# Low parts of 32 chunks of u made early, kept in DRAM, and moved by GpSimd's queue

## The chip, the cores and the metric

The kernel runs on one core of a Trainium2 chip. The metric is the time of one execution in microseconds of the device, from the runs shown below. The engines are TensorE (PE, its weight loads PEld), VectorE (DVE), ScalarE (ACT), GpSimd (POOL) and SyncE (SP), which only issues transfers. Each engine takes its instructions from a queue in a fixed order and waits at the head of it. GpSimd, ScalarE and SyncE can also issue DMAs from their queues.

## What is computed

Two blocks of a transformer for 512 tokens of width 1024, all in float32. The first block has a mixer (latent attention and retention, both gated and merged) and then a PEER layer: each token picks 16 experts of 16384 in each of 8 heads, by a top-16 over two sets of 128 keys, and adds up what they give. The second block has an attention with three branches and an ordinary feed-forward layer. The lines that matter here are

```python
merged = jax.nn.sigmoid(za) * y_a + jax.nn.sigmoid(zr) * y_r     # the merges
...
act = jax.nn.gelu(jnp.einsum('td,tkd->tk', xt, peer_u[it]), approximate=False)
return jnp.einsum('tk,tkd->td', gt * act, peer_v[it])
```

## The kernel before

**Products in three passes.** Float32 accuracy is kept by cutting each operand into a high part `h` in the reduced float32r type and a low part `l`, the remainder. A product is three matmul passes: high by high, high by low, low by high (`fm`, L256 for its matmuls). `weights` (L224) fetches a weight tile of 128 x 1024 by SP's queue into `wr`; `split` (L210, L211) makes `wh` by a cast on ScalarE and `wl` by a subtract, on VectorE or GpSimd. `wr`, `wh` and `wl` have two buffers each. For the mixer's weights (`wfm`) the subtract goes to GpSimd every second time.

**The merges.** For each of the 8 chunks of 128 output columns the loop before L860 makes four products: the gate `w_za`, the attention's `w_mla` (half as long), the gate `w_zr`, the retention's `w_ret`. `merged` then adds the two gated results (L856, GpSimd), and makes the high and low part of half the sum (ScalarE, VectorE). The residual product `w_mix` and the query products follow.

**Routing, with early fronts beside it.** PEER is computed for all experts: 128 chunks of 128 experts. For the first 384 tokens a `front` multiplies one chunk of `u` with the tokens (24 matmuls) and takes the gelu; later a chunk of `v` is multiplied with the gated activations. The last 128 tokens are done apart, by gathering the rows of `u` and `v` with indirect DMAs on GpSimd. 72 of the 128 fronts stand beside the routing: VectorE finds the top 16 and writes one-hot tables (`topk`, `spread`, L928 to L1096), ScalarE scales them, TensorE multiplies them (L1101) into the gate table, which goes to DRAM. `step` (PACE, LEAD) sets how many fronts have been traced after each step of the routing. In these fronts the chunk's low part is always made by GpSimd:

```python
def front(e, u=None):
    u = u or u_of(e, G)
```

From front 72 on, fronts alternate with the products of `v`, in a loop whose order on three engines is written out by hand; there the low part is VectorE's.

**What sets the order.** In the merges and in the routing, the order of each engine's queue is laid out when the program is built, by a planner that walks through the traced instructions with costs of its own, puts an instruction into its engine's queue when its inputs and its tile are ready there, and prefers what was traced earlier. On the chip the queues are then followed as they are. A tile's buffer is handed on when its last reader has finished.

Of the kernel before, what the change touches and what calls it, by code (L numbers as in the profile page):

```python
# [9 lines left out]
F32 = mybir.dt.float32  # L10
F32R = mybir.dt.float32r
# [3 lines left out]
OP = mybir.AluOpType  # L15
AX = mybir.AxisListType

P = 128
# [4 lines left out]
D = 1024  # L23
KD = D // P
# [142 lines left out]
def build(tc, A, OUT):  # L167
    nc = tc.nc
    es = ExitStack()
    V, S, G, TE = nc.vector, nc.scalar, nc.gpsimd, nc.tensor  # L170

    def pool(name, bufs=1, stack=es, **kw):
        if kw.get("space") != bass.MemoryType.DRAM:
            kw["reuse_waits"] = "tile"
        return stack.enter_context(tc.tile_pool(name=name, bufs=bufs, **kw))

    cp = pool("cst")
    dp = pool("dram", space=bass.MemoryType.DRAM)
# [10 lines left out]
    def mmps(name="mm"):  # L189
        return bank("mm", name)  # L190
# [17 lines left out]
    def split(src, hi, lo, lo_eng=None):  # L208

        S.copy(hi, src)  # L210
        (lo_eng or V).tensor_tensor(lo, src, hi.bitcast(F32), op=OP.subtract)  # L211
# [6 lines left out]
    def load(ap, n, tag="w", queue=nc.sync):  # L218
        wp, words, bufs = wts[tag]
        raw = wp.tile([P, words], F32, name=tag + "r", bufs=bufs)  # L220
        queue.dma_start(raw[:, :n], ap)
        return raw

    def weights(ap, n, lo_pool=3, tag="w", raw=None):  # L224

        wp, words, bufs = wts[tag]
        raw = raw or load(ap, n, tag)
        hi = wp.tile([P, words], F32R, name=tag + "h", bufs=2)
        lo = wp.tile([P, words], F32R, name=tag + "l", bufs=2)
        flip[0] += 1  # L230
        if isinstance(lo_pool, int):
            lo_pool = V if flip[0] % lo_pool else G
        split(raw[:, :n], hi[:, :n], lo[:, :n], lo_pool)
        return hi, lo

    def kview(pair, kt, width):
        return tuple([t[:, k * width:(k + 1) * width] for k in range(kt)] for t in pair)
# [55 lines left out]
    def ks(t):  # L293

        return [t[:, k] for k in range(t.shape[1])]
# [131 lines left out]
    def two(tp, name="t2", dt=F32):  # L427

        return tp.tile([P, L], dt, name=name, tag="t2")
# [4 lines left out]
    def halves(name, tag, dt=F32):  # L434
        h = [xp.tile([P, 4, L], dt, name=name, tag=tag, bufs=2) for _ in range(2)]
        return h, [h[k // 4][:, k % 4] for k in range(KD)]
# [18 lines left out]
    def half_slot(name, dt=F32):  # L455
        return sp_.tile([P, 4, L], dt, name=name, tag="h")

    def flat(t, n):
        return t.rearrange("p k t -> p (k t)")[:, :n]

    def mtwo(name="m2"):
        return tp.tile([P, L], F32, name=name, tag="m2", bufs=9)

    src = A["hT"].rearrange("p (k t) -> p k t", k=KD)
    _, h1 = halves("h1", "xa")
# [56 lines left out]
    c = ks(half_slot("ckv", F32R))  # L522
# [6 lines left out]
    x = mtwo()  # L529
# [8 lines left out]
    for t0, t1, m in ((0, NT, P), (NT, NT + 1, M)):  # L538
        h = t1 - t0
        pv = pt[:m, t0 * 32:t1 * 32].rearrange("p (t d) -> p t d", t=h)  # L540
        x = mtwo()
# [84 lines left out]
    for h in range(8):  # L626
        b = 64 - h % 2 * 64
# [4 lines left out]
    def fm_pieces(w, pieces):  # L632

        x = two(t2)
        for a, b in pieces:
            ps = mmps()
            fm(ps[:, :b - a], w, hn, 0, a, b - a)
            S.copy(x[:, a:b], ps[:, :b - a])
        return x
# [110 lines left out]
    for h in range(8):  # L750
        x = fm_pieces(wfm("w_rv", h), PIECES)
# [10 lines left out]
        b = h % 2 * 64  # L762
# [65 lines left out]
    for h in range(8):  # L828
        w = wfm("w_rg", h)
# [10 lines left out]
    def gate(name, c, x):  # L840

        w = wfm(name, c)
        ps = mmps()
        fm(ps, w, hn, 0, 0, T)
        S.activation(x, ps, AF.Tanh, scale=0.5)
        return x

    def gated(name, c, act, kt, x):

        w = wfm(name, c, kt)  # L850
        ps = mmps()
        fm(ps, w, act, 0, 0, T, kt)
        V.scalar_tensor_tensor(x, x, 1.0, ps, op0=OP.add, op1=OP.mult)

    def merged(a, b, mg, d):
        G.tensor_tensor(a, a, b, op=OP.add)  # L856
        S.activation(mg[0][d], a, AF.Copy, scale=0.5)
        V.scalar_tensor_tensor(mg[1][d], a, 0.5, mg[0][d].bitcast(F32), op0=OP.mult, op1=OP.subtract)

    mg = tuple([x for _ in range(2) for x in ks(half_slot(n, F32R)[:, :, :T])] for n in ("mgh", "mgl"))  # L860
    for c in range(KD):
        x = gate("w_za", c, two(t2)[:, :T])
        gated("w_mla", c, oT, 4, x)
        y = gate("w_zr", c, two(t2)[:, :T])
        gated("w_ret", c, yr, KD, y)
        merged(x, y, mg, c)
    sty.close()
    h1 = [x for _ in range(2) for x in ks(half_slot("h1"))]
# [69 lines left out]
    acts, done_u = {}, []  # L938

    def u_of(e, eng=V):  # L940
        return kview(weights(A["u_T"][e], D, eng), KD, P)

    def act_tile(e, side):
        return (tr if side else tp).tile([P, TD], F32, name="act", bufs=15 if side else 19)
# [381 lines left out]
    for x in range(2):  # L1326
# [8 lines left out]
        for hf in range(2):  # L1335
            w = sp_.tile([P, 8, 256], F32, name="wc1", tag="h")
            nc.sync.dma_start(w.rearrange("p l c -> p (l c)"), A["w_c1"][x][:, hf * 2048:(hf + 1) * 2048])
            w1.append(w)
    for br in range(2):
        w = wfm("w_kv", 2 * br)  # L1340
# [4 lines left out]
        for g in range(2):  # L1345
            a, b = slice(g * 64, g * 64 + 64), slice(64 - g * 64, 128 - g * 64)
# [4 lines left out]
        w = wfm("w_kv", 2 * br + 1)  # L1351
        ps = mmps()
        fm(ps, w, hn, 0, 0, T)
        x = two(t2)[:, :T]
# [8 lines left out]
    w = wfm("w_gn", 0, width=48)  # L1363
# [3 lines left out]
    x = two(t2)[:48, :T]  # L1367
# [158 lines left out]
    for g in range(4):  # L1526
        w = wfm("w_u", g)
# [32 lines left out]
    for c in range(KD):  # L1560
        y = gate("w_gm", KD + c, two(t2)[:, :T])
        gated("w_pn", c, ysl, KD, y)
        x = gate("w_gm", c, two(t2)[:, :T])
# [19 lines left out]
    w = kview(weights(A["w_f1"][0], KD * 256, tag="ww"), KD, 256)  # L1583
# [11 lines left out]
    for b in range(4):  # L1595
        f = tuple(ks(slot(n, F32R)) for n in ("fh", "fl"))
        for c in range(4):
            if b or c:
                w = kview(weights(A["w_f1"][4 * b + c], KD * 256, tag="ww"), KD, 256)
# [52 lines left out]
```

## Time and profile before

| what | value |
|---|---|
| time, median of 3 runs | 2685.57 us (2683.2 to 2687.15) |
| the profiled execution | 2681.29 us |
| its span | 2679.5 us |
| TensorE busy | 2585.8 us, 97% |
| VectorE, ScalarE, GpSimd busy | 1702.9, 1146.1, 926.6 us |
| moved by DMA | 465.80 MB |

The span is what the profile covers; the execution takes 1.8 us more. TensorE's matmuls overlap and their ends are modelled, so that its busy share is no measure of how much room is left; waits and the chain of waits are. The merges fill about 344 to 500 us of the span, the routing about 605 to 1014, the fronts with the products of `v` follow to about 1805, and then comes the second block.

### The profile page before, as it was taken

To read this page: it belongs to the slowest core of one execution; us is meant where nothing else is said; L and a number is where in the kernel's file an instruction comes from. 1 tells how busy PE (TensorE), PEld (TensorE's weight loads), DVE (VectorE), ACT (ScalarE), POOL (GpSimd) and SP (SyncE) were. 2 spreads that over 40 slices of the span, in tenths; PEclk is the share of its full clock that TensorE was granted. 3 is DMA by queue.
4 is the path that set the end of the run, shared out by engine and by line. 5 is a ranking of instruction groups with operands and counts; after the bars stand their busy time and mean duration, and the time that the engine had idled before them with its cause. 6 is when DMAs were issued, how large, how long until landed. Compare 5 with 4: busy or idle time off the path is not lost.

```text
span 2679.5 us, 37137 instructions
## 1 busy us (share of the span) xinstructions
PE 2585.8 (97%) x13809; PEld 2225.1 (83%) x13809; DVE 1702.9 (64%) x3399; ACT 1146.1 (43%) x2097; POOL 926.6 (35%) x590
## 2 busy tenths in 40 slices
PE   8899999999899999999999999999999999899998
PEld 7768778899899988888888888887666788787887
DVE  5772442246998992898989888866778412534333
ACT  5552342244577663333333333334667422422322
POOL 2122122325344342565555555522222233211112
PEclk9999999999999999999999999998999999999999
DMA  3322223323356568999999999963110122222221
GB/s 129 100 69 68 67 75 122 119 84 118 103 174 195 168 199 290 331 368 400 402 408 370 339 351 333 337 203 108 53 43 25 60 95 96 109 94 95 94 95 63
DMA packets 177957, 465.80 MB, mean 174 GB/s; under 512 B 15856, under 2 KB 78960, under 8 KB 171120
## 3 DMA queue, kind: packets, MB, share of 16 engines
q1 hardware_dynamic: 136736, 322.84, 34.7%
q0 software_dynamic: 36864, 134.23, 13.6%
q10 hardware_dynamic: 4176, 6.36, 0.8%
q8 instruction: 108, 1.77, 0.3%
q14 instruction: 73, 0.60, 0.1%
HBM read 421.17 MB, written 37.42 MB: 171 GB/s over the span
## 4 chain that ended last, share of the span: by engine, by line
PE 78%; DVE 14%; ACT 2%; DMA 2%; issue 2%; POOL 1%; ACTq 1%; SPq 0%; DVEq 0%; POOLq 0%
PE mm L256 36%; PE py L1182 19%; PE pu L256 13%; DVE oh L1093 3%; PE o L1510 2%; PE tp L1505 1%; DMA t<-t 1%; PE mm L1101 1%; DVE xn L350 1%; DVE oh L1065 1%; DVE oh L1068 1%; DVE oh L1096 1%; PE s L699 1%; DVE ef L1070 1%; DMA wr<-in_u_T_dram 1%
## 5 line engine op out<-in xcount | busy, mean ns | idle before, releaser
L211 POOL TENSOR_TENSOR wl<-wr,wh 128x1024 fp32r<-128x1024 f32 (+1 forms) x142 | 349.9, 2465 | 764.5 <-ACT wh L210 329.5
L210 ACT CAST wh<-wr 128x1024 fp32r<-128x1024 f32 (+2 forms) x271 | 273.4, 1010 | 311.2 <-PE mm L256 203.4
L256 PE MATMUL pu<-xf,wh 128*128 128x384 f32 x2048 | 392.3, 343 | 10.3 <-ACT wh L210 5.8
L256 PEld LDWEIGHTS pu<-xf,wh 128*128 128x128 f32 x2048 | 362.0, 190 | 16.3 <-ACT wh L210 6.2
L211 DVE TENSOR_TENSOR wl<-wr,wh 128x1024 fp32r<-128x1024 f32 (+2 forms) x129 | 152.0, 1179 | 184.0 <-ACT wh L210 112.2
L974 POOL DMA_INDIRECT row<-in_v_rows_dram,eg x128 | 195.7, 1529 | 163.7 <-DVE yg L989 136.9
L974 POOL DMA_INDIRECT row<-in_u_rows_dram,eg x128 | 187.8, 1467 | 176.2 <-DVE row L979 155.1
L256 PE MATMUL pu<-xf,wl 128*128 128x384 f32 x1024 | 202.4, 339 | 2.6 <-POOL wl L211 2.6
L1169 ACT CAST ah<-act 128x384 fp32r<-128x384 f32 x128 | 65.8, 514 | 324.0 <-DVE act L1166 302.2
L1182 PE MATMUL py<-vl,ah 128*128 128x512 f32 x768 | 195.8, 389 | 0.1
L1182 PE MATMUL py<-vh,ah 128*128 128x512 f32 x768 | 195.7, 389 | 0.0
L1182 PE MATMUL py<-vh,al 128*128 128x512 f32 x768 | 195.6, 389 | 0.0
L256 PEld LDWEIGHTS pu<-xf,wl 128*128 128x128 f32 x1024 | 182.5, 189 | 3.5 <-POOL wl L211 3.5
L1174 DVE TENSOR_TENSOR vl<-vr,vh 128x1024 fp32r<-128x1024 f32 x128 | 156.3, 1221 | 22.3 <-ACT vh L1172 22.3
L1182 PEld LDWEIGHTS py<-vl,ah 128*128 128x128 f32 x768 | 144.0, 188 | 30.6 <-DVE vl L1174 0.7
L1182 PEld LDWEIGHTS py<-vh,al 128*128 128x128 f32 x768 | 144.2, 188 | 30.0
L989 DVE SCALAR_TENSOR_TENSOR yg<-row,ag,yg 128x1024 f32<-128x1024 f32 x127 | 162.9, 1282 | 5.3 <-DMA row<-in_v_rows_dram,eg 2.9
L1182 PEld LDWEIGHTS py<-vh,ah 128*128 128x128 f32 x768 | 143.3, 188 | 25.4
L979 DVE SCALAR_TENSOR_TENSOR row<-row,xg 128x1024 f32<-128x1024 f32 x128 | 152.3, 1221 | 9.9 <-DMA row<-in_u_rows_dram,eg 9.9
L1093 DVE TENSOR_TENSOR oh<-iota,eT 128x1024 f32<-128x1024 f32 x96 | 139.8, 1483 | 14.0 <-PE mm L1101 12.6
L381 DVE TENSOR_TENSOR h<-mm,h 128x512 f32<-128x512 f32 (+1 forms) x54 | 34.1, 632 | 172.6 <-PE mm L256 172.6
L1172 ACT CAST vh<-vr 128x1024 fp32r<-128x1024 f32 x128 | 134.6, 1051 | 19.5 <-PE py L1182 18.7
(468 smaller groups left out, 5103.3 us busy)
## 6 DMA issues: line engine op xcount, KB each, us to landing
wr<-in_u_T_dram SPq DMA_DIRECT2D x128, 512.0 KB
vr<-in_v_rows_dram SPq DMA_DIRECT2D x128, 512.0 KB
wwr<-in_w_f_dram SPq DMA_DIRECT2D x32, 1024.0 KB
gates<-stg SPq DMA_DIRECT2D x24, 1024.0 KB
gin<-gates SPq DMA_DIRECT2D x16, 1536.0 KB
wr<-in_w_gm_dram SPq DMA_DIRECT2D x16, 512.0 KB
ahead<-act SPq DMA_DIRECT2D x41, 192.0 KB
act<-ahead SPq DMA_DIRECT2D x41, 192.0 KB
```

What stands on the lines that cost most here:

```text
L210: S.copy(hi, src)
L211: (lo_eng or V).tensor_tensor(lo, src, hi.bitcast(F32), op=OP.subtract)
L256: TE.matmul(out, w[a][k][:, c0:c0 + P], act[b][k][:, t0:t0 + n], start=i == 0 and k == 0, stop=i == 2 and k == kt - 1)
L974: G.indirect_dma_start(out=r, out_offset=None, in_=src, in_offset=bass.IndirectOffsetOnAxis(ap=eg[:, k:k + 1], axis=0))
L979: V.scalar_tensor_tensor(r, r, 1.0, xg, op0=OP.mult, op1=OP.mult, accum_out=ag[:, k:k + 1])
L989: V.scalar_tensor_tensor(yg[0], r, ag[:, k:k + 1], yg[0], op0=OP.mult, op1=OP.add)
L1093: V.tensor_tensor(a1, iota[:, None, None, :].to_broadcast([P, 2, 4, P]), eT[:, :2, b0 + q0:b0 + q0 + 4, None].to_broadcast([P, 2, 4, P]), ...
L1169: S.copy(ah, a)
L1172: S.copy(vh, raw)
L1174: V.tensor_tensor(vl, raw, vh.bitcast(F32), op=OP.subtract)
L1182: TE.matmul(py[2 * t + d], x[:, t * P:(t + 1) * P], w[:, d * 512:(d + 1) * 512], start=e == 0 and i == 0, stop=e == P - 1 and i == 2)
L1510: TE.matmul(po[b * 64:b * 64 + 64, :2 * P], vt[:, j, br, g], pT[:, b * 256:b * 256 + 256], start=False, stop=last, skip_group_check=True)
```

## The change

For the 32 even chunks 0, 2, ... 62 of `u`, the low part is made during the merges and stored in DRAM (`ulow`, 32 x 512 KB). Four staging buffers are used: each holds a chunk and, beside it, its high part. `low_load` fetches a chunk on GpSimd's queue; `low_part` casts it (ScalarE), subtracts (VectorE), stores the remainder to `ulow` on GpSimd's queue, and fetches the chunk four further on into the same buffer. One `low_part` stands behind each of the four products of a merge round. In `front`, `weights` then takes the low part of these chunks from `ulow`, by a DMA on GpSimd's queue, in place of the subtract; the chunk itself is still fetched and cast. The add in `merged`, which both blocks use, goes from GpSimd to VectorE.

```diff
-    def weights(ap, n, lo_pool=3, tag="w", raw=None):
+    def weights(ap, n, lo_pool=3, tag="w", raw=None, low=None):
...
+        if low is not None:
+            G.dma_start(lo.bitcast(F32)[:, :n], low)
+            S.copy(hi[:, :n], raw[:, :n])
+            return hi, lo
...
     def merged(a, b, mg, d):
-        G.tensor_tensor(a, a, b, op=OP.add)
+        V.tensor_tensor(a, a, b, op=OP.add)
...
+    NLOW = 32
+    low_of = {2 * j: j for j in range(NLOW)}
+    ulow = dp.tile([NLOW, P, D], F32, name="ulow")
...
+    stage = [flat(x, 2 * D) for x in halves("stage", "xa")[0] + [half_slot("stage") for _ in range(2)]]
+
+    def low_load(j):
+        G.dma_start(stage[j % 4][:, :D], A["u_T"][2 * j])
+
+    def low_part(j):
+        raw, hi = stage[j % 4][:, :D], stage[j % 4][:, D:].bitcast(F32R)
+        S.copy(hi, raw)
+        V.tensor_tensor(raw.bitcast(F32R), raw, hi.bitcast(F32), op=OP.subtract)
+        G.dma_start(ulow[j], raw)
+        if j + 4 < NLOW:
+            low_load(j + 4)
+
+    for j in range(4):
+        low_load(j)
     for c in range(KD):
         x = gate("w_za", c, two(t2)[:, :T])
+        low_part(4 * c)
         gated("w_mla", c, oT, 4, x)
+        low_part(4 * c + 1)
         y = gate("w_zr", c, two(t2)[:, :T])
+        low_part(4 * c + 2)
         gated("w_ret", c, yr, KD, y)
+        low_part(4 * c + 3)
         merged(x, y, mg, c)
...
     def u_of(e, eng=V):
-        return kview(weights(A["u_T"][e], D, eng), KD, P)
+        return kview(weights(A["u_T"][e], D, eng, low=ulow[low_of[e]] if e in low_of else None), KD, P)
```

## Rows read from the trace of the kernel before

**Rows 1.** Chain that ended last, shares of the span by engine and by line.

```profile
PE 78%; DVE 14%; ACT 2%; DMA 2%; issue 2%; POOL 1%; ACTq 1%; SPq 0%; DVEq 0%; POOLq 0%
PE mm L256 36%; PE py L1182 19%; PE pu L256 13%; DVE oh L1093 3%; PE o L1510 2%; PE tp L1505 1%; DMA t<-t 1%; PE mm L1101 1%; DVE xn L350 1%; DVE oh L1065 1%; DVE oh L1068 1%; DVE oh L1096 1%; PE s L699 1%; DVE ef L1070 1%; DMA wr<-in_u_T_dram 1%
```

**Rows 2.** Busy us by stretch: length, PE, PEld, DVE, ACT, POOL, clock, DMA share, GB/s.

```profile
344.50:500.40 155.90, 154.74 (x686) 125.01 (x685) 43.01 (x68) 50.15 (x67) 42.11 (x26) 1.00 0.31 103
605.00:1014.00 409.00, 388.48 (x2430) 382.60 (x2429) 360.28 (x982) 252.67 (x561) 179.82 (x67) 0.98 0.54 163
1300.00:1500.00 200.00, 200.00 (x960) 175.71 (x960) 179.32 (x236) 72.97 (x99) 111.93 (x76) 1.00 1.00 385
```

**Rows 3.** Waits of PE, 605 to 1045: total us, times, longest.

```profile
PE tp L1079 <- DVE ef L1070: 6.8, 1, 6.8
PE pu L256 <- ACT wh L210: 5.8, 1, 5.8
PE mm L1101 <- ACT oh L1098: 4.7, 6, 1.8
PE pu L256 <- ACT act L961: 4.4, 4, 1.7
PE pu L256 <- POOL wl L211: 2.6, 2, 2.4
PE mm L1101 <- DVE oh L1096: 2.0, 4, 0.6
```

**Rows 4.** PE in order of time in the routing: start, us, instructions merged.

```profile
609.96 2.96 PE L256 MATMUL pu<-xf,wh 128*128 128x384 f32 x16
612.75 1.57 PE L256 MATMUL pu<-xf,wl 128*128 128x384 f32 x8
614.16 2.96 PE L256 MATMUL pu<-xf,wh 128*128 128x384 f32 x16
...
684.11 4.26 PE L256 MATMUL pu<-xf,wh 128*128 128x384 f32 x15
```

**Rows 5.** GpSimd's subtract, 605 to 1014: by line, and ns min/median/max.

```profile
L211 POOL TENSOR_TENSOR wl<-wr,wh 128x1024 fp32r<-128x1024 f32 x67 | 180.4, 2693 | 229.6 <-ACT wh L210 134.3 <-PE pu L256 57.0 <-PE mm L1101 29.5
L211 POOL TENSOR_TENSOR wl<-wr,wh x67: 2361/2402/5736, 604.5 to 1011.6; 128x1024 fp32r<-128x1024 f32 x67
```

**Rows 6.** VectorE by line, 605 to 1014: busy us, mean ns, idle before.

```profile
L1093 DVE TENSOR_TENSOR oh<-iota,eT 128x1024 f32<-128x1024 f32 x96 | 139.8, 1483 | 14.0 <-PE mm L1101 12.6 <-ACT oh L1098 1.5
L1096 DVE TENSOR_SCALAR oh<-oh,eT 128x128 f32<-128x128 f32 x64 | 30.0, 526 | 0.0
L1068 DVE TENSOR_TENSOR oh<-oh,idf 128x1024 f32<-128x1024 f32 x16 | 22.7, 1425 | 0.0
```

**Rows 7.** The same lines of VectorE: ns min/median/max, first and last start.

```profile
L1093 DVE TENSOR_TENSOR oh<-iota,eT x96: 1198/1214/3429, 688.2 to 1003.9; 128x1024 f32<-128x1024 f32 x96
L1096 DVE TENSOR_SCALAR oh<-oh,eT x64: 263/278/2435, 913.1 to 1005.4; 128x128 f32<-128x128 f32 x64
```

**Rows 8.** GpSimd's indirect gather of 128 rows of u: ns min/median/max.

```profile
L974 POOL DMA_INDIRECT row<-in_u_rows_dram,eg x128: 936/1673/1989, 1014.2 to 1395.1; - x128
```

**Rows 9.** SP's queue in order of time: loads of u, start and us.

```profile
604.01 3.18 SPq L221 DMA_DIRECT2D wr<-in_u_T_dram  x2
...
1021.15 2.97 SPq L221 DMA_DIRECT2D wr<-in_u_T_dram  x2
```

**Rows 10.** ScalarE in order of time: the casts that waited for these loads.

```profile
608.98 1.05 ACT L210 CAST wh<-wr 128x1024 fp32r<-128x1024 f32 x1 [4.33 <-DMA wr<-in_u_T_dram]
...
1033.01 1.04 ACT L210 CAST wh<-wr 128x1024 fp32r<-128x1024 f32 x1 [3.27 <-DMA wr<-in_u_T_dram]
```

**Rows 11.** By line, 344.5 to 500.4, engines ACT, DVE, POOL.

```profile
L210 ACT CAST wh<-wr 128x1024 fp32r<-128x1024 f32 x24 | 25.2, 1050 | 40.1 <-PE mm L256 36.3 <-DMA wr<-in_w_za_dram 3.8
L211 DVE TENSOR_TENSOR wl<-wr,wh 128x1024 fp32r<-128x1024 f32 x15 | 18.4, 1225 | 45.2 <-PE mm L256 45.2
L856 POOL TENSOR_TENSOR t<-t,t 128x512 f32<-128x512 f32 x7 | 9.1, 1295 | 0.0
```

## The prediction

> **What bounds the kernel now.** I read the chain of waits first [rows 1]: TensorE holds 78% of it and VectorE 14%, and the VectorE lines in it (L1093, L1065, L1068, L1096, L1070) all belong to one stage, the routing with the 72 early fronts. Then I cut the span into the two stages that the change touches [rows 2]. During the merges (344.5 to 500.4) TensorE is busy for 154.7 of 155.9 us at a granted clock of 1.00, while GpSimd works 42 us, ScalarE 50, VectorE 43, and the DMA engines have a share of 0.31. So the merges are TensorE's, 155.9 / 8 = 19.5 us for each of eight rounds, with much room beside it. In the routing stage (605 to 1014) TensorE is busy 388.5 of 409 us and VectorE 360.3: two engines that lead in turn. What TensorE waits for there stands in [rows 3]. Leaving out the 5.8 us that come from the crowded hand-over to the next stage, it is 6.8 + 4.7 + 4.4 + 2.6 + 2.0 = 20.5 us, and nearly all of it is lateness of VectorE, or of ScalarE work queued behind VectorE. After a wait TensorE also runs slowly for a moment: 15 matmuls take 4.26 us behind the 6.8 us wait where 16 take 2.96 otherwise [rows 4]; such places add perhaps 5 us. Some 25 us is thus the most that this stage can give back. Everything from 1045 on is full of TensorE work and untouched.
>
> **What the routing stage gains.** The GpSimd subtract that makes a chunk's low part runs 67 times there, 180.4 us [rows 5], and VectorE is slowed by it. L1093 has a median of 1214 ns and a maximum of 3429: the difference of 2215 is about one GpSimd subtract (2402) [rows 5, 7]. Taking each line's total less its count times the median, for L1068 that of L1093, whose shape it has [rows 6, 7]: L1093 139.8 - 96 x 1.214 = 23.3; L1096 30.0 - 64 x 0.278 = 12.2; L1068 22.7 - 16 x 1.214 = 3.3. Together 39 us at least, since smaller lines that suffer too are left out. Of the 67 subtracts about 30 belong to even chunks up to 62 and disappear, so VectorE loses 30/67 x 39 = 17 us less. TensorE can use that only where it waits for it. The 6.8 us wait comes early (676), when VectorE has gained perhaps 3 us; the rest (13.7 us) comes later, when it is ahead by more than any of these waits is long. 3 + 13.7 is nearly 17 us. Bounds: 0, if the waits only move, and 25. I take 15 gross.
>
> The Trainium skill, in SBUF — State Buffer, section "Who interferes with whom", calls the port pair that GpSimd and VectorE share an exclusive lock: a VectorE operation with two inputs in SBUF, or one in a two-port mode, blocks for the whole GpSimd instruction that reads SBUF. The trace agrees (2215 ns lost against a subtract of 2402). The same page says that descriptor writing for GpSimd's DMAs is locked out by two-port VectorE operations; by that the new low transfers could be held by L1096's 278 ns each, 30 x 0.28 = 8 us at worst if each met one.
>
> **What is put in its place there.** Each of the 32 low parts is now a transfer on GpSimd's queue into the `l` tile. No plain DMA of GpSimd is in the trace; the nearest row is its indirect gather of the same 512 KB, 936 to 1989 ns of GpSimd time, median 1673 [rows 8]. Bounds for one issue: 0 (nothing that stands in the way of other work) to 2.0 us; I take 1.67, less than the 2.4 of the subtract. The landing: a load of u issued by SP at 604.01 lets ScalarE cast at 608.98, 4.9 us later in a quiet stretch; in the crowd at 1021.15 it took until 1033.01, 11.9 us [rows 9, 10]. Like the subtract, the transfer must wait until the front two before it has ended, since there are two `l` tiles. While fronts run back to back (4.2 us each, [rows 4]) there are 4.2 + 2.8 = 7.0 us until the third group of matmuls needs it; 1.67 + 4.9 = 6.6 fits by 0.4. Later the 72 fronts share 440 us, 6.1 us each, and there are over 10. What is queued behind the waiting transfer on GpSimd is the subtract for the next odd chunk, which waits for a later front anyway. Bounds: 0 to 32 x 1 us of TensorE waits; I take 3, in the first 70 us. The `wr` tile of an even chunk comes free earlier, after the cast alone, so SP can only issue sooner. Net gain of the stage 15 - 3 = 12 us.
>
> **What the merges pay.** Added in eight rounds: 32 loads and 32 stores on GpSimd's queue, 32 casts on ScalarE (1050 ns), 32 subtracts on VectorE (1225), and the add of each merge moves from GpSimd (1295) to VectorE, where half a subtract's row makes about 0.7 [rows 11]. ScalarE: 50 + 34 = 84 of 156 us. VectorE: 43 + 39 + 6 = 88. GpSimd: 42 - 9 + 64 x 1.67 = 140 of 156, the fullest of the three, and that counts no waiting. DMA: 64 x 524 KB = 33.6 MB in 155.9 us is 215 GB/s; at the 385 GB/s that goes with a share of 1.00 in [rows 2] this is 0.56, on top of 0.31: 0.87.
>
> A round has four low parts and there are four staging buffers, so the stream keeps up as long as one buffer's turn is under 19.5 us: issue 1.67, land 4.9, cast 1.05, subtract 1.23, issue 1.67, land 4.9 = 15.4. It fits, with 4 us over. The waits that come in: a cast waits for its load at the head of ScalarE's queue, and behind it stand the weights' casts and the tanh that empties TensorE's bank; a store waits for the subtract at the head of GpSimd's queue, and the load behind it waits until that store has landed; behind those stands every second weight's low part. The order in these queues is laid out beforehand, so what decides is by how much the transfers land later than it assumes. ScalarE's casts of weights mostly stood waiting for TensorE to free a tile (36.3 of 40.1 us idle, [rows 11]), so a microsecond of lateness is absorbed. Bounds: 0 (all in the room beside TensorE) to 8 x (29.4 - 19.5) = 79 us with both landings at the crowded 11.9. I take 4, near the quiet landing, since the share stays under 1. If that cover goes, the price falls on TensorE in full.
>
> The Trainium skill, in DMA: Bandwidth & Descriptors, section "Issuing engines are not separate DMA queues", speaks against the change: DMAs of all queues run on the same 16 engines and interleave. By that the weights' loads of SP are slowed by the low stream, which the 0.87 already assumes; with separate engines the 4 us would be 0.
>
> The tiles of h1 now come free only after the last w_mla, since two staging buffers hold their place; 2.1 MB at 385 GB/s are 5.4 us, and a w_ret product and the first w_mix product, some 11 us, cover them. If not, the first residual sums are a few us late. The second block's adds move to VectorE as well, in a stage of TensorE: 0. The FFN's weights alternate from another start, with as many on GpSimd give or take one: 0.
>
> **Sum.** -12 + 4 = -8 us against the profiled execution, whose span of 2679.5 takes 2681.3 in all; the median of the runs shown is 2685.57, 4.3 above, and the same 8 us taken from it give 2677.5.
>
> **Rivals.** *The low stream holds up the merges.* With landings of 8.4 us, halfway between the two rows, a buffer's turn is 22.4, and 8 x (22.4 - 19.5) = 23 us are lost; GpSimd, at 140 of 156, adds its own head-of-queue waits, some 7. 30 - 12 gives +18: 2703.5. It decides once a turn exceeds 19.5 us. For it: DMA share 0.87, three queues that wait in order. Against it: every sum still fits. *The gain is used up in the fronts.* If the low part needs 8.2 us instead of 6.6, eight even fronts in the back-to-back stretch lose 1.2 each, 10 us, and -12 shrinks to about -2 plus the 4: within 0.2%, 2683 to 2688. The same comes out if TensorE's waits only move to the next thing that is late. *All waits go*, 20.5 plus the slow moments after, merges at no cost: -20, 2665.5. That the change doesn't do what it says I hold excluded: the subtracts of these chunks are not issued.
>
> **How the numbers follow.** About 0.2%, 5.4 us, is what a measurement of this kernel can tell from no change. Forecast 0.40 (own range 2668 to 2680), all waits go 0.07, gain used up 0.21, merges held up 0.32. So faster 0.47, same 0.21, slower 0.32. The range reaches from 2664 to 2710; beyond it lie the worst landings.
>
> **What would show it.** Right: L1093's mean falls from 1483 towards 1350; some 37 GpSimd subtracts of 1024 in the routing stage; TensorE's wait for L1070 at half its 6.8 us or less; the merges still at 19.5 us a round with a DMA share near 0.87. Wrong: waits of TensorE for wh or for its bank during the merges, ScalarE waiting for the staging loads, the merges ending more than 10 us after 500; or waits of the third group of matmuls of even fronts for the DMA into `wl`.

## The result, and the profile after

The changed kernel takes 2708.49 us (median of 4 runs, 2706.03 to 2712.71), the kernel before 2684.78 beside it (4 runs, 2683.2 to 2687.15): ratio 1.0093, 95% interval 1.0081 to 1.0105. It is slower by 24 us where 8 us of gain were forecast. The profiled span is 2704.3 us, 24.8 above that of before.

Two stretches tell where the time went. From the first `w_mla` matmul to the first `w_mix` matmul (I call this the merges) the timeline of TensorE shows 341.73 to 500.39 before and 340.28 to 536.64 after: 158.7 became 196.4 us, +37.7. From the first front to the first product of `v` (the routing) it shows 605.57 to 1044.72 and 641.87 to 1067.97: 439.2 became 426.1, -13.1. From there to the end, and before 340, nothing differs by more than 2 to 3 us. So the gain came as forecast, and the merges took three times as much.

Changed kernel, three stretches (us, then busy time and count on TensorE, its weight loads, VectorE, ScalarE, GpSimd; granted clock, DMA share, GB/s); they answer to [rows 2]:

```profile
344.50:520.00 175.50, 150.65 (x624) 118.66 (x623) 86.70 (x113) 76.64 (x96) 65.02 (x79) 0.93 0.77 263
...
641.80:1068.00 426.20, 408.95 (x2556) 404.85 (x2556) 334.15 (x987) 264.36 (x575) 137.71 (x76) 0.98 0.69 220
...
384.00:484.00 100.00, 83.33 (x329) 65.13 (x327) 50.46 (x48) 42.92 (x51) 39.08 (x52) 0.92 0.91 309
```

In the merges TensorE, busy all the time in [rows 2], now stands 25 of 175 us idle, and its clock falls to 0.93. No other engine is near full: 87, 77 and 65 of 175 us. Only the DMA share is high, 0.91 in the middle. What waits for what, 330 to 620 (us in total, times, longest):

```profile
ACT stage L876 <- DMA stage<-in_u_T_dram: 56.5, 23, 4.0
DVE stage L877 <- ACT stage L876: 53.7, 22, 3.9
...
POOL stage L872 <- DMA ulow<-stage: 41.8, 19, 5.5
...
POOL ulow L878 <- DVE stage L877: 20.7, 10, 5.3
...
PE mm L260 <- ACT t L849: 12.8, 4, 6.1
...
PE mm L260 <- DVE t L857: 4.3, 2, 3.7
```

The first four lines are those of the low stream (cast, subtract, load, store): each waits at the head of its queue for the one before it. The last two lines are what reaches TensorE: the tanh and the gated product that empty its bank. One instance in order of time, ScalarE first, then TensorE (start, us, instruction, in brackets the idle time before it and what ended it):

```profile
479.76 1.04 ACT L876 CAST stage<-stage 128x1024 fp32r<-128x1024 f32 x1 [2.70 <-DMA stage<-in_u_T_dram]
480.71 1.04 ACT L210 CAST wh<-wr 128x1024 fp32r<-128x1024 f32 x1
482.83 1.04 ACT L876 CAST stage<-stage 128x1024 fp32r<-128x1024 f32 x1 [1.08 <-DMA stage<-in_u_T_dram]
483.79 0.59 ACT L849 ACTIVATE t<-mm 128x512 f32<-128x512 f32 x1
```

```profile
473.71 1.78 PE L260 MATMUL mm<-hnh,wl 128*128 128x512 f32 x7
...
477.19 1.09 PE L260 MATMUL mm<-oTh,wl 128*128 128x512 f32 x4
484.43 3.78 PE L260 MATMUL mm<-hnh,wh 128*128 128x512 f32 x8 [6.15 <-ACT t L849]
488.01 2.37 PE L260 MATMUL mm<-hnl,wh 128*128 128x512 f32 x8
490.21 2.02 PE L260 MATMUL mm<-hnh,wl 128*128 128x512 f32 x8
```

The gate's product is done at 475.5 (the `hnh,wl` line). In ScalarE's queue two casts of the stream stand ahead of its tanh, each waiting for its load, and the tanh runs at 483.79. TensorE stands for 6.15 us, and then does eight matmuls in 3.78 us that take 2.02 otherwise. TensorE's waits in this stretch (the two lines above, and 3.7, 2.2 and 1.8 us beside the last chunks of the retention, which still run in the first round) make 24.8 us, against 1.8 in the kernel before:

```profile
PE tp L813 <- DVE ry L809: 1.3, 2, 0.7
PE mm L256 <- ACT t L845: 0.5, 1, 0.5
```

Slower matmuls make some 11 of the rest: 120 of `hnh,wh` with a mean of 440 ns and 120 of `hnl,wh` with 430, where an undisturbed one takes 397, are 9.1 us, and those of `w_mla` add 2.4.

The routing, to be held against [rows 3] and [rows 5 to 7]; TensorE's waits, 640 to 1070:

```profile
PE pu L260 <- POOL wl L211: 6.8, 3, 3.2
PE pu L260 <- ACT wh L210: 5.8, 1, 5.8
PE tp L1106 <- DVE ef L1097: 4.7, 1, 4.7
```

and groups by line (busy us, mean ns, idle before):

```profile
L1120 DVE TENSOR_TENSOR oh<-iota,eT 128x1024 f32<-128x1024 f32 x96 | 136.2, 1445 | 26.2 <-PE mm L1128 22.3 <-ACT act L988 3.7
...
L1123 DVE TENSOR_SCALAR oh<-oh,eT 128x128 f32<-128x128 f32 x64 | 18.2, 343 | 0.0
...
L260 PEld LDWEIGHTS pu<-xf,wl 128*128 128x128 f32 x576 | 103.1, 191 | 8.3 <-POOL wl L211 7.8 <-DMA wl<-ulow 0.5
```

Without the hand-over (5.8, as before) TensorE waits 11.5 us instead of 20.5. For the fetched low tiles it waits 0.5 us in all, in the queue of its weight loads (the last line).

### The profile page after: what moved, and what is told of

Read it like the earlier page. It is cut to its first block, busy times and chain, and to the rows that moved or that the text cites. A ratio compares the mean times of both kernels' runs of the same rounds, so it can differ in the third digit from the quotient of the medians.

```text
span 2704.3 us, 37327 instructions
## 1 busy us (share of the span) xinstructions
PE 2598.1 (96%) x13809; PEld 2233.4 (83%) x13809; DVE 1728.1 (64%) x3447; ACT 1180.3 (44%) x2131; POOL 880.3 (33%) x638
## 4 chain that ended last, share of the span: by engine, by line
PE 81%; DVE 6%; DMA 5%; issue 3%; POOL 2%; ACT 2%; ACTq 1%; DVEq 0%; POOLq 0%; SPq 0%
PE mm L260 32%; PE py L1209 18%; PE pu L260 18%; PE mm L1128 3%; DMA stage<-in_u_T_dram 2%; PE o L1537 2%; POOL wl L211 1%; PE tp L1532 1%; DMA ulow<-stage 1%; DMA t<-t 1%; PE s L703 1%; DVE xn L354 1%; DMA wr<-in_u_T_dram 1%; ACT wh L210 1%; PE ssq L285 0%
## 5 line engine op out<-in xcount | busy, mean ns | idle before, releaser
L211 POOL TENSOR_TENSOR wl<-wr,wh 128x1024 fp32r<-128x1024 f32 (+1 forms) x110 | 274.9, 2499 | 714.6 <-ACT wh L210 290.0
L210 ACT CAST wh<-wr 128x1024 fp32r<-128x1024 f32 (+2 forms) x239 | 240.1, 1006 | 253.9 <-PE mm L260 175.2
L1201 DVE TENSOR_TENSOR vl<-vr,vh 128x1024 fp32r<-128x1024 f32 x128 | 156.2, 1220 | 22.5 <-ACT vh L1199 22.5
L1006 DVE SCALAR_TENSOR_TENSOR row<-row,xg 128x1024 f32<-128x1024 f32 x128 | 152.3, 1220 | 7.3 <-DMA row<-in_u_rows_dram,eg 7.2
L1120 DVE TENSOR_TENSOR oh<-iota,eT 128x1024 f32<-128x1024 f32 x96 | 136.2, 1445 | 26.2 <-PE mm L1128 22.3
L1199 ACT CAST vh<-vr 128x1024 fp32r<-128x1024 f32 x128 | 134.6, 1052 | 19.5 <-PE py L1209 18.9
```

The costliest lines, as they stand in the source:

```text
L1006: V.scalar_tensor_tensor(r, r, 1.0, xg, op0=OP.mult, op1=OP.mult, accum_out=ag[:, k:k + 1])
L1120: V.tensor_tensor(a1, iota[:, None, None, :].to_broadcast([P, 2, 4, P]), eT[:, :2, b0 + q0:b0 + q0 + 4, None].to_broadcast([P, 2, 4, P]), ...
L1199: S.copy(vh, raw)
L1201: V.tensor_tensor(vl, raw, vh.bitcast(F32), op=OP.subtract)
```

## The experiments

**What they had to tell apart.** Theory T: the casts of the stream stand at the head of ScalarE's in-order queue, waiting for loads, and hold up what TensorE needs; it grew in two steps, told below (T2 in the expectations is T with the dense order that the planner gives these casts). Rivals: the traffic itself (a DMA share of 0.9 delays the weights); GpSimd's single queue, in which loads stand behind stores and the weights' subtracts behind both; the engine time of 32 casts and subtracts. All times stand beside the kernel before in the same runs (2682 to 2685 us).

| kernel | ratio to before (95%) | merges, us | routing, us |
|---|---|---|---|
| before | 1 | 158.7 | 439.2 |
| changed | 1.0093 (1.0081 to 1.0105) | 196.4 | 426.1 |
| fronts alone | 0.9957 (0.9941 to 0.9974) | 158.6 | 423.8 |
| merges alone | 1.0134 (1.0117 to 1.0151) | 196.6 | 436.7 |
| loads on SyncE | 1.0076 (1.0059 to 1.0093) | 192.7 | 425.9 |
| 32 on GpSimd | 1.0065 (1.0048 to 1.0082) | 168.5 | 425.9 |
| 16, dense | 1.0030 (1.0020 to 1.0039) | 173.9 | 431.1 |
| no stores | 1.0017 (1.0007 to 1.0027) | 180.2 | 426.3 |
| 24 on GpSimd | 1.0082 (1.0065 to 1.0099) | 183.9 | 431.8 |
| 24 paced, 4 buffers | 0.9993 (0.9983 to 1.0002) | 161.2 | 430.4 |
| 32 paced, 4 buffers | 1.0085 (1.0072 to 1.0099) | 192.3 | 426.1 |
| 28 paced, 4 buffers | 1.0046 (1.0032 to 1.0060) | 170.0 | 427.4 |
| 24 paced in 6 rounds | 1.0027 (1.0016 to 1.0039) | 168.1 | 430.7 |
| 28 paced, 6 buffers | 0.9976 (0.9963 to 0.9989) | 158.1 | 427.8 |
| 28 paced, 4, later load | 1.0068 (1.0055 to 1.0081) | 187.6 | 427.1 |
| 32 dense, 6 buffers | 1.0078 (1.0063 to 1.0092) | 193.3 | 426.5 |
| 32 dense, 6, `wl` on VectorE | 1.0042 (1.0028 to 1.0056) | 184.9 | 424.7 |
| 32 paced, 6, `wl` on VectorE | 0.9962 (0.9948 to 0.9975) | 159.5 | 424.8 |
| **32 paced, 6 buffers** | **0.9962 (0.9949 to 0.9975)** | 160.6 | 426.1 |

**Each half by itself.** First the fronts' part without the stream:

```diff
-    for j in range(4):
-        low_load(j)
+    for k in range(2):
+        nc.sync.dma_start(ulow[0][:, k * T:(k + 1) * T], hn[0][k].bitcast(F32)[:, :T])
...
-        low_part(4 * c)
...
-        low_part(4 * c + 1)
...
-        low_part(4 * c + 2)
...
-        low_part(4 * c + 3)
...
-        return kview(weights(A["u_T"][e], D, eng, low=ulow[low_of[e]] if e in low_of else None), KD, P)
+        return kview(weights(A["u_T"][e], D, eng, low=ulow[0] if e in low_of else None), KD, P)
```

> The 32 low parts are not made: two plain transfers fill one low tile in DRAM once (with other data, so the low parts of these chunks are wrong), and the fronts fetch it as in the changed kernel; nothing but the merged add is added to the merges. Queue theory (the whole loss comes from the stream in the merges): the routing stage keeps its gain of 13 us and the merges cost nothing, 2672 us against 2685, first w_mix product at 500 us in the trace. Rival, the fetches in the fronts cost what they save and the loss is elsewhere: 2685 or more.

2670.31 us against 2681.91: -11.6, with the merges at 158.6. So the whole loss comes from the stream, and the merged add on VectorE costs nothing. Then the stream, never read (`low=None` in the fronts):

> The low parts are made beside the merges and never read; the fronts subtract on GpSimd as in the kernel before. If the two stages add up: the merges lose their 36 us and the routing stage takes the 439 us of before, so 2685 + 36 = 2721. If the loss in the merges is part of a later recovery (work only moved ahead), less: under 2710.

2718.77, +36.9. The two stages add up (-11.6 + 36.9 = 25.3 against the 24 measured).

**Which queue.** The loads on SyncE (`nc.sync.dma_start` in `low_load`):

> The 32 staging loads are issued by SyncE's queue, the stores stay on GpSimd's. Rival G (GpSimd's single queue, in which a load stands behind the wait of a store and the weights' subtracts behind both, is the cause): most of the 36 us in the merges goes, about 2680. Theory T (ScalarE's and VectorE's in-order queues, where the casts of late loads hold back the tanh and the weights' casts): a load can still not start before its buffer's store has landed, so the casts go on waiting, TensorE's waits for the tanh stay, 2695 to 2710. SyncE's queue may then also hold weights' loads behind a staging load: up to 2725.

2703.69; the merges get back 3.7 of 37.7 us, so taking the loads out of the shared queue is no cure. ScalarE still waits 49.1 us for staging loads. The comparison is not clean: the planner lays out every kernel anew, and here it put 31 casts ahead of the ninth tanh where the changed kernel has 26. Then cast and subtract on GpSimd:

```diff
-        S.copy(hi, raw)
-        V.tensor_tensor(raw.bitcast(F32R), raw, hi.bitcast(F32), op=OP.subtract)
+        G.tensor_copy(hi, raw)
+        G.tensor_tensor(raw.bitcast(F32R), raw, hi.bitcast(F32), op=OP.subtract)
```

> The same 64 transfers, but the cast and the subtract of each low part run on GpSimd, so that ScalarE and VectorE never wait for a staging transfer; in the merges all the weights' low parts go to VectorE. Theory T: TensorE's waits for the tanh and the gated product vanish, the merges end within 5 us of 500, total about 2675. Rival B (the traffic itself delays the weights): the same bytes, so most of the 36 us stays, 2700 or more. GpSimd alone may fail to finish 32 parts in 156 us; then the rest runs on beside w_mix and nothing waits for it before the first fronts at 606.

2700.84, which looks like the rival; the trace says otherwise. TensorE, 384 to 484 and then in order of time:

```profile
384.00:484.00 100.00, 97.19 (x411) 77.80 (x410) 59.29 (x40) 26.98 (x35) 69.54 (x61) 0.98 0.74 247
```

```profile
519.29 2.02 PE L261 MATMUL mm<-mgl,wh 128*128 128x512 f32 x8
541.51 3.78 PE L261 MATMUL mm<-mgh,wl 128*128 128x512 f32 x8 [20.20 <-POOL wl L212]
```

The merges lose 9.8 us in place of 37.7 with the stream still running. The rest lies behind them (from the first `w_mix` matmul to the first front 130.4 us in place of 105.2) and is one wait of 20.2 us with slow matmuls after it: GpSimd had not finished its 32 parts, and the first low part of `w_mix` given to it stood behind them. The loss had moved to another queue's head. With 24 parts, the loads started later and the weights' low parts kept off GpSimd until `w_mix` is done:

> 24 parts, cast and subtract on GpSimd, the first loads not before the first gate of the merges, and all low parts of weights on VectorE until w_mix is done. T: the merges and w_mix lose under 4 us in all, three quarters of the routing's gain remain (9 us): 2675. Rival (the 9 us lost in the first rounds of the kernel with cast and subtract on GpSimd came from the traffic or from VectorE sharing its port, not from the overlap with the retention chunks): 2682 or more.

A miss: 2704.85. SyncE's waits, then ScalarE and TensorE in order of time:

```profile
SPq L900 <- DMA ulow<-stage: 22.1, 2, 18.5
```

```profile
504.95 1.04 ACT L211 CAST wh<-wr 128x1024 fp32r<-128x1024 f32 x1 [20.83 <-DMA wr<-in_w_za_dram]
```

```profile
506.55 3.46 PE L261 MATMUL mm<-hnh,wh 128*128 128x512 f32 x8 [12.27 <-ACT t L850]
```

A load of `h1`, whose place a staging buffer still held, waited 18.5 us at the head of SyncE's queue for a store, and the gate weights' load behind it came 20 us late. A third queue, the same pattern. It makes 13.9 of the 25.2 us that the merges lose here (the last round takes 33.4 us in place of 19.5). The other 11, like the 9.8 of the kernel before it, fall in earlier rounds; TensorE waits 6.3 us there for VectorE's part in the retention. Whether the traffic or VectorE's work beside GpSimd's makes them is not shown.

**Engine time, traffic or order.** The order of ScalarE's queue in the changed kernel, as laid out when the program is built, has 2, 5, 9, 12, 15, 17, 20, 23, 26, 28, 32 casts of the stream ahead of the 1st to 11th of sixteen tanh. That is 5.75 a round between the third and the eleventh, not the four of the text: I take it that the planner counts a buffer as free again much sooner than it is. Four buffers at 5.75 parts a round (4 x 19.5 / 5.75) would have to turn in 13.6 us; measured from one store to the next store of the same buffer, a turn in this kernel takes 18.4 us on average (28 turns, 14.5 to 25.8). With that the sum closes: the stream passes a part every 4.8 us (32 from 330 to 485), 5.75 of them take 27.6 us, and the rounds from 391 to 496 last 24.2 to 27.9 us in place of 19.5; the two rounds behind the last cast take 19.5 again. Half the parts:

```diff
-    NLOW = 32
+    NLOW = 16
...
-        low_part(4 * c)
+        low_part(2 * c)
...
-        low_part(4 * c + 1)
...
-        low_part(4 * c + 2)
+        low_part(2 * c + 1)
...
-        low_part(4 * c + 3)
```

> 16 low parts instead of 32, two behind each merge round in the program's text; everything else as in the changed kernel. The forecast's measure (a buffer's turn against the time in which its next part is due, now 39 us): no loss at all, half the gain, 2682 - 6 = 2676. Theory T2 (the planner lays the parts into ScalarE's queue as densely as its own landing times allow, six or seven casts per round whatever the text says, so every part still waits): the loss goes with the number of parts, 16 x 1.13 = 18 us, so 2682 + 18 - 6 = 2694, and all of it in the first three or four rounds.

2691.27, and the merges lose 15.2 us, all before 425. The order has the same dense start, then no more casts. The measure by which I had forecast no loss is wrong here. Without the stores:

```diff
-        G.dma_start(ulow[j], raw)
+        if j == 0:
+            G.dma_start(ulow[j], raw)
```

> Only the first low part is stored; the other 31 loads, casts and subtracts are made as in the changed kernel, and the fronts fetch the one stored part (so the low parts of 31 chunks are wrong). The load no longer waits for a store's landing, and the stream's traffic is halved. Forecast's measure (the turn, now about 9 us): no loss, 2670. Theory T2 (the casts at the head of ScalarE's queue wait for landings later than planned): the planner packs the casts still closer, each still waits for its load, and a good part of the 36 us stays: 2680 to 2695. If the 64 us of casts and subtracts themselves were the price: 2700.

2689.24; merges +21.5. The planner now puts all 32 casts ahead of the seventh tanh, and they still wait 18.5 us for loads. Half the bytes of the stream do not free it. The share is 0.56 between 384 and 484, but 0.75 up to 430, while the casts run, so that this run tells less of the traffic than its bytes suggest.

Then the pace: a one-column copy ahead of each cast, into the place where the cast will write, from a result of the cast's own round. The queue can't hold the cast earlier than that.

```diff
-    def low_part(j):
+    def low_part(j, x):
...
+        S.copy(hi[:, :1], x[:, :1])
         S.copy(hi, raw)
```

With 24 parts, three per round, and `wl` of the merges' weights all on VectorE:

> Casts on ScalarE and subtracts on VectorE as in the changed kernel, but 24 parts, three per round, and each cast is tied to a result of its own round by a one-column copy ahead of it, so that the queue can't hold it earlier; all low parts of the merges' weights go to VectorE. T2: loads have landed when the casts come up, TensorE's waits in the merges shrink to under 5 us, 2682 + 4 - 9 = 2677. Rival (engine time of ScalarE and VectorE or the traffic is the price): 24 x 1.13 = 27 us stay, 2700.

2682.37, and TensorE loses nothing once the retention chunks are done:

```profile
384.00:484.00 100.00, 100.00 (x433) 80.94 (x432) 51.83 (x56) 46.16 (x66) 16.61 (x31) 1.00 0.74 262
```

VectorE and ScalarE are as busy in this stretch as in the changed kernel (51.8 and 46.2 against 50.5 and 42.9 us), so engine time is not the price. The traffic is lower, 0.74 against 0.91; that rival waits for a later kernel. The total is still that of before: in the trace the merges and the routing together gain 6.3 us, and the stretches before, between and behind them lose 8 (4.0 of them behind the routing), which I did not follow further. But pace alone, on the changed kernel with its 32 parts:

> The changed kernel with one edit: a one-column copy on ScalarE ahead of each of the 32 casts, taking a result of the cast's own merge round, so that each round holds four casts and no more. T2 (the dense order in ScalarE's queue is the cause): the merges lose under 12 us in place of 36, 2682 + 12 - 13 = 2681 or less. Rival (32 turns through four buffers and GpSimd's queue can't be had in eight rounds whatever the order): the casts still wait for their loads, 2700.

A miss for T as I held it then: 2707.59, no better than the changed kernel. Its waits, 330 to 545:

```profile
POOL stage L872 <- DMA ulow<-stage: 86.0, 24, 6.0
...
ACT wh L210 <- DMA wr<-in_w_mla_dram: 36.7, 6, 8.1
...
PE mm L260 <- POOL wl L211: 21.6, 8, 6.0
...
ACT stage L877 <- DMA stage<-in_u_T_dram: 3.8, 4, 2.7
```

The casts' waits for loads have gone from 56.5 us to 3.8. GpSimd's loads wait 86 us for stores instead, the weights' subtracts behind them are late, and TensorE waits for these. Its rounds last 24.3 us (the last `w_ret` matmuls of three rounds begin at 457.44, 481.71 and 505.98). The rival set against T there, that 32 turns through four buffers and GpSimd's queue can't be had in eight rounds, has its time come true, though not by casts that wait for loads.

**The turn of a buffer.** Two kernels with `wl` on VectorE and four paced parts per round, in rounds 1 to 7 and 1 to 6:

> 28 parts, four per round in rounds 1 to 7, each cast tied to its round, all low parts of the merges' weights on VectorE. T2: the rounds beside the retention chunks are spared, the loss is that of 24 paced parts without its 3 us at the start, 1 to 4 us if a turn of four buffers still fits in 19.5 us; the routing keeps 28/32 of 13 us: 2672 to 2676. If the turn no longer fits: a wait of the casts for their loads in every round, 2685.

> As the kernel with 28 parts, but 24 parts in rounds 1 to 6, so that the last round and the residual product have no staging buffer and no cast in their way. T2: merges within 2 us of the kernel before, the routing keeps 10 of 13 us: 2674. Against the kernel with 28 parts: if the last round costs it over 2 us, this one is the faster.

2696.41 and 2690.19, both misses. The first loses 11.3 us in the merges and 11.6 behind them, where its last cast (526.18) stands ahead of the half-sum that a `w_mix` product waits 8.3 us for. GpSimd's queue in the first of them, in order of time; `ulow` are the stores, in the order of the parts, so that every fourth is of the same buffer:

```profile
430.86 0.54 POOL L880 DMA_DIRECT2D ulow<-stage  x1
438.08 0.53 POOL L873 DMA_DIRECT2D stage<-in_u_T_dram  x1 [6.68 <-DMA ulow<-stage]
438.60 0.54 POOL L880 DMA_DIRECT2D ulow<-stage  x1
444.47 0.53 POOL L873 DMA_DIRECT2D stage<-in_u_T_dram  x1 [5.33 <-DMA ulow<-stage]
444.99 1.07 POOL L880 DMA_DIRECT2D ulow<-stage  x2
451.87 0.54 POOL L873 DMA_DIRECT2D stage<-in_u_T_dram  x1 [5.81 <-DMA ulow<-stage]
454.73 0.54 POOL L873 DMA_DIRECT2D stage<-in_u_T_dram  x1 [2.33 <-DMA ulow<-stage]
455.26 0.54 POOL L880 DMA_DIRECT2D ulow<-stage  x1
462.09 0.53 POOL L873 DMA_DIRECT2D stage<-in_u_T_dram  x1 [6.29 <-DMA ulow<-stage]
462.61 0.54 POOL L880 DMA_DIRECT2D ulow<-stage  x1
```

From 430.86 to 455.26 and from 438.60 to 462.61 a buffer's turn is 24.4 and 24.0 us. The first can be followed through the queues. The load behind the store waits for it and goes out at 438.08, 7.2 us after the store's issue; then come ScalarE's cast and VectorE's subtract of this part:

```profile
443.02 1.05 ACT L878 CAST stage<-stage 128x1024 fp32r<-128x1024 f32 x1 [2.10 <-DMA stage<-in_u_T_dram]
...
444.10 1.23 DVE L879 TENSOR_TENSOR stage<-stage 128x1024 fp32r<-128x1024 f32 x1 [2.63 <-ACT stage L878]
```

The load takes 4.9 us to the cast, cast and subtract 2.3, and from 445.33 to 455.26 the finished part stands 9.9 us in GpSimd's queue, behind loads that wait for other stores. Over this kernel's 24 turns the mean is 23.6 us, 7.8 of them this standing; in the changed kernel it is 1.9 of 18.4.

A round is 19.5 us. Three parts per round leave 26 us a turn, four leave 19.5; 24 parts in eight rounds fit, four per round do not. Two readings agree with this. One is the turn. The other is GpSimd's queue alone: 23 waits for a store make 116.7 us, 5.1 each, and with the two issues (0.54 each) a part holds the queue for some 6.2 us, four of them for 24.6. As four parts share four buffers, a turn is as long as a round in either case, so the 24 us don't decide between them. Six buffers at four per round leave 29 us a turn, and a load, still issued four parts ahead, then goes into a buffer that was stored two parts before, so that it need not wait for the store just ahead of it. The four tiles of staging hold eight halves:

```diff
+    eight = [x[:, k * D:(k + 1) * D] for x in stage for k in range(2)]
+    raws, his = eight[:6], eight[6:]
...
-        raw, hi = stage[j % 4][:, :D], stage[j % 4][:, D:].bitcast(F32R)
+        raw, hi = raws[j % len(raws)], his[j % len(his)].bitcast(F32R)
...
         if j + 4 < NLOW:
+            G.tensor_copy(raws[(j + 4) % len(raws)][:, :1], x[:, :1])
             low_load(j + 4)
```

> 28 parts, four per round in rounds 1 to 7, paced as in the kernel with 28 parts before; the four staging tiles are cut into six for the chunk and two for the high part, and a load is issued four parts ahead into a buffer whose store went out two parts before. A turn is now 6/4 x 19.5 = 29 us. Theory turn, and theory GpSimd's queue: no cast waits for its load any more, rounds stay at 19.5 us, 2673 to 2677. Rival traffic (share 0.85 delays weights and loads alike): the 15 us of the four-buffer kernel stay, 2690 to 2697.

2677.51, faster than before, at a DMA share of 0.87:

```profile
384.00:484.00 100.00, 100.00 (x433) 80.96 (x432) 59.36 (x63) 52.50 (x77) 35.06 (x61) 1.00 0.87 310
```

With four buffers and a load issued one part later:

> The same 28 parts and pace with four buffers for the chunk, but the load of a buffer is issued one part (4.9 us) after its store, so that GpSimd's queue doesn't wait for the store's landing at its head. Theory GpSimd's queue: the waits of loads for stores (117 us with 28 parts) go, and with them the loss, 2673 to 2678. Theory turn: a turn is still 19.5 us, a load has 14.6 us less the store's lateness, casts wait again, 2685 to 2695. Rival traffic: 2690 to 2697.

2702.25, but it doesn't settle what it was made for. The one-column copy on GpSimd reads the gate's tile, which VectorE then overwrites, and so it tied the two together:

```profile
DVE t L858 <- POOL stage L884: 53.9, 10, 11.8
```

Which of the two readings limits four buffers, the turn or GpSimd's queue, stays open; six buffers relieve both.

**Both needed?** Six buffers in the planner's dense order, with `wl` split as in the changed kernel, and with `wl` on VectorE; then six buffers, paced, 32 parts, with `wl` on VectorE and split:

> The changed kernel with one edit: six buffers for the chunk and two for the high part in the same four tiles, no pacing; the casts stand in ScalarE's queue where the planner puts them (about 13 to 14 in the rounds up to the third tanh pair, all 32 before the seventh round). If the turn of the buffers alone limits: 6 buffers at a turn of 19 to 24 us pass a part every 3.2 to 4 us, 32 parts in 102 to 128 us, which the planned six rounds (117 us) nearly hold: 2672 to 2685. If the dense order is a cause of its own (casts planned for landings of 2 us wait at the head whatever the buffers): 2690 to 2705.

> 32 parts, six buffers, the planner's dense order, but all low parts of the merges' weights on VectorE, so that GpSimd's queue holds only the staging transfers. If the subtracts on GpSimd, waiting for ScalarE's high parts in front of loads and stores, were what kept the six-buffer kernel slow: 2671 to 2680. If the dense order in ScalarE's queue is enough by itself (32 casts before the eleventh tanh of sixteen): casts still wait for loads, 2690 to 2703.

> As the six-buffer kernel with 28 paced parts, with all 32 in rounds 0 to 7. Theory turn: 4 more parts are worth 1.6 us in the routing; the first round beside the retention chunks costs about 2 to 3 us, as with 24 paced parts from round 0: 2676 to 2680, no better than 28 parts.

> 32 parts, six buffers, paced casts and loads issued four parts ahead, but every second low part of the merges' weights stays on GpSimd, as in the changed kernel. If pace and buffers are enough: 2672 to 2677. If GpSimd's queue must be free of other work: waits of TensorE for the weights' low parts, as in the paced kernel with four buffers, 2685 to 2705.

Dense: 2704.51 and 2697.31. Paced: 2673.94 and 2674.83, the first better than expected (no worse than 28 parts). The stretch from 384 to 484 of the first (dense, split) and of the last (paced, split):

```profile
384.00:484.00 100.00, 78.44 (x313) 60.98 (x311) 49.56 (x44) 40.23 (x47) 35.93 (x50) 0.92 0.87 296
```

```profile
384.00:484.00 100.00, 100.00 (x433) 80.93 (x432) 55.13 (x52) 54.05 (x77) 52.81 (x73) 1.00 0.91 315
```

Same buffers, same queues, same kind of work; the share is higher in the one that loses nothing. In the dense kernel ScalarE waits 48.8 us for staging loads; in the paced one 1.5:

```profile
ACT stage L879 <- DMA stage<-in_u_T_dram: 48.8, 22, 4.3
```

```profile
ACT stage L880 <- DMA stage<-in_u_T_dram: 1.5, 2, 1.0
```

Yet the transfers of the paced kernel are not quick. From 384 to 484 its 21 staging loads and its 21 stores read

```profile
DMA to landing us min/median/max: 4.4/6.2/7.1
...
DMA to landing us min/median/max: 4.4/6.3/7.1
```

Buffers without pace lose 22 us, pace without buffers 24; with both (the pace here also ties each load, issued four parts ahead, to its round) the change gains: 2674.83 against 2684.57, and 2673.94 against 2682.95, ratio 0.9962 each. These beat both kernels. Six buffers with the casts tied but not the loads, or the loads but not the casts, were not tried.

## Why the prediction was wrong

**The routing stage: right in size, half right in way.** -12 was forecast, -13.1 is measured, and -11.6 in total time with the fronts alone. The early wait for L1070 fell from 6.8 to 4.7 us, not to half. L1093's mean fell to 1445 ns, not 1350; L1096, now L1123, fell more, from 526 to 343. VectorE is busy 334.2 us in the routing in place of 363.9 (605.5 to 1044.7 of before), 30 us less, where I had 17. TensorE's waits fell by 9.0 us, where I took 15 gross; what it still waits for is above all the odd chunks' subtract on GpSimd (6.8 us). The price of the fetches in the fronts is 0.5 us, not 3: a fetch's issue takes GpSimd 0.57 us, not 1.67, and the landing was covered. All 32 issues took 567 to 573 ns, so that the 8 us which the prediction allowed for VectorE holding them up did not come. The gain was thus not used up in the fronts; that -12 and -13.1 lie so close is in part luck, since their terms do not.

**The merges: the failed step.** "It fits, with 4 us over" and "I take 4, near the quiet landing, since the share stays under 1". Measured: 37.7. Three things were wrong in it, the first above all.

- The pace. "A round has four low parts" I took from the program's text. ScalarE's order has 5.75, so the limit for a turn was 13.6 us and not 19.5, and my own sum of 15.4 does not fit it. The measured turn of 18.4 us is under 19.5, and the loss came all the same; with the loads on SyncE the turn is 15.8 us, close to my sum, and the merges lose 34.0. I had written that what decides is by how much the transfers land later than the order assumes, and then did not size it.
- The terms of a turn. I had 15.4 us: two issues of 1.67, two landings of 4.9, cast and subtract. The issues are 0.54; in the paced kernel with the share at 0.91 the landings are 6.2 and 6.3 us (median), which with 2.3 for cast and subtract makes 14.8. So the sum of these pieces was about right. What it put at nothing is the standing in queues between them: once four parts per round are held to, with four buffers, the turn is 24 us, some 8 of them in GpSimd's queue. The point of decision of the first rival, 19.5 us, is one for the paced kernels, not for the changed one.
- The cover. "A microsecond of lateness is absorbed" because ScalarE stands waiting for TensorE: true of one wait, but each round has five or six casts of the stream, and ScalarE waits 56.5 us for their loads in 23 waits, ahead of a tanh with nothing in reserve. From there the price falls on TensorE in full, with slower matmuls after each wait, as the text said it would if that cover went.

The rival "the low stream holds up the merges" came true, though not by its landings of 8.4 us, and through ScalarE's queue more than GpSimd's; I gave it 0.32. Its 2703.5 was 5 short of 2708.5, since its 30 us were 37.7 in the trace.

**Traffic.** The rule that transfers of all queues share the same engines (the Trainium skill, DMA: Bandwidth & Descriptors, "Issuing engines are not separate DMA queues") was cited against the change. That transfers land later beside others fits it (6.2 us at a share of 0.91, 4.9 for one load in a quiet stretch). No run here shows the lateness to cost TensorE anything by itself: at a share of 0.91 the paced kernel keeps TensorE busy for 100.00 of 100 us. It was the in-order queues that made lateness dear.

**h1 and the second block**: no loss seen in the changed kernel, from the first `w_mix` matmul to the first front 105.2 us as before; in the kernel with 24 parts on GpSimd the `h1` loads did become the block. The marks set for "wrong" were the ones that appeared: TensorE waiting for its bank in the merges, ScalarE for staging loads, the merges ending 36 us after 500.

## What to carry to other kernels

Work laid into the idle time of engines beside a full TensorE cost nothing here for its busy time or its traffic; the whole price lay in waits at the head of a queue that TensorE needs. Read from the order, not from the program's text, how many such instructions stand ahead of the one that frees the bank, and compare the turn of their buffers with that. Two things were needed together: enough buffers for the pace that the stream is to keep, and a tie of each consumer to the stage it belongs to, so that a planner can't pull it ahead of its data. When a cure only moves the loss to another queue (ScalarE, GpSimd, SyncE, in turn here), the total time looks like a dead theory; the waits show that it isn't.

## What the runs showed of the hardware

- Issuing a plain 512 KB transfer holds GpSimd for 0.53 to 0.57 us (medians in the changed kernel; the longest 0.76); its indirect gather of the same size took 1.67 [rows 8].
- Transfers of 512 KB on GpSimd's queue at a share of 0.91 land 6.2 us (loads) and 6.3 us (stores) after their issue, 4.4 to 7.1, against 4.9 for a load in a quiet stretch [rows 9, 10]. The longest flight of a store in the kernel with 28 parts and four buffers is 9.8 us (477.45 to 487.26, at a share of 0.81).
- With cast and subtract of the stream on GpSimd, VectorE's subtract of weights in the merges takes 1212 to 5495 ns, median 1966 (32, seven of them half as wide); in the changed kernel it takes 1192 to 1323, median 1220 (16, all of full width). VectorE is slow beside a busy GpSimd, as its L1093 is in [rows 7].
- After the wait of 6.15 us the granted clock falls to 0.50, the lower of its two levels (1.2 GHz), which is why eight matmuls take 3.78 us instead of 2.02; some us later it is 1.00 again. Changed kernel, columns as above:

```profile
484.50:487.50 3.00, 3.00 (x7) 2.41 (x8) 1.24 (x2) 0.81 (x1) 2.05 (x2) 0.50 1.05 421
492.00:512.00 20.00, 20.00 (x87) 16.18 (x87) 5.86 (x7) 5.85 (x8) 3.71 (x2) 1.00 0.40 140
```
